# Two transformer blocks on one core: keys of block 2 transposed once a pair and spread by DMA, and 21 weight rests moved to VectorE

## The chip, the core and the metric

The kernel runs on one core of a Trainium2 chip. The time is the device time of one launch in microseconds (us), as the median of several runs. A core has five engines that run their own instruction lists and wait for each other by semaphores: TensorE (PE, matrix products and transposes; PEld is its weight load), VectorE (DVE), ScalarE (ACT), GpSimd (POOL) and SyncE (SP, which here only issues DMA transfers). PE writes to PSUM, from which ACT and DVE bring results to SBUF.

## The reference, cut to what matters

Two transformer blocks of width 1024 work on 512 positions, each with its own weights and with two layers. In the second block, which the change is mostly about, a layer is a pool mixer beside a top-k attention with an index, an output product and an MLP:

```python
def second_block(x, positions, ...):
    for l in range(DEPTH):
        h = rms_norm_2(x, g_pre_mix[l])
        proj = h @ w_in[l]
        u_pool, q, k, v, iq, ik, iw = jnp.split(proj, SPLIT_POINTS, axis=-1)
        q, k, iq, ik = ...                      # rotary positions
        a_out = pool_mixer(u_pool, w_pool[l], pool_scale[l])
        b_out = dsa_attention(q, k, v, iq, ik, iw, topk)
        mix = jnp.concatenate([a_out, b_out], axis=-1) @ w_out[l]
        x = x + rms_norm_2(mix, g_post_mix[l])
        h = rms_norm_2(x, g_pre_ffn[l])
        f = jnp.square(jax.nn.relu(h @ w_ff1[l])) @ w_ff2[l]
        x = x + rms_norm_2(f, g_post_ffn[l])
```

`dsa_attention` has 8 heads of 64. The index scores (`iq`, `ik`, `iw`) choose 128 keys for each query, and each head takes a softmax over these alone. The kernel computes all scores and adds a bias that shuts out the others. The first block has a differential attention beside a recurrent unit, an MLP and a gated product; of it the change touches only the first weights that are converted, at the kernel's start.

## The kernel before

**Numbers in two parts.** PE multiplies in a reduced 32-bit format, so each operand is kept as a rounded part (`hi`, for weights `wh`) and the rest (`lo`, `wl`), and a product is the sum of hi x hi, hi x lo and lo x hi.

**Weights.** `PLAN` lists the pieces of all weights in the order of use, most of them 128x1024. `w_load` (L191) brings a piece by SP into one of three buffers `raw`. `w_conv` (L193) converts it three pieces ahead of its use: ACT makes `wh` (L206), and the rest is made in one of three ways. For pieces of the names in `ON_POOL` and the list `BY_DMA`, ACT writes `-wh` to `wl` (L212) and GpSimd issues a DMA that adds the weight to it from memory (L215). For pieces 1 to 5 GpSimd subtracts in two halves (L219). For all others VectorE subtracts (L131 in the profile, like all of its work). `index` has the weights of the index projection, whose kept pieces are named `F` in layer 1, and `w_out_2` those of the output product; its pieces with `k` from 4 multiply the attention's own heads and come last.

**Block 2's attention.** `mix2` works on four pairs of heads, `j` = 0 to 3. Queries and keys lie as `qk`, four tiles of 128 positions. A score tile is a product of a stacked query `qs` (hi of a head in 64 rows, lo in the other 64) with `ks`, whose two halves hold the key's hi and its lo, each of them twice, in rows 0 to 63 and 64 to 127. `prep_q` transposes the queries of a pair on PE (four transposes, `tpose4`) and stacks them. For keys, `prep_d` lets GpSimd copy a head's 64 columns twice side by side into a tile `xe` (`twice`, L624, four copies a head), and `prep_k` transposes it (`dups`, four transposes a head), ACT copies hi (L634), DVE subtracts lo.

**Order.** PE runs in the order in which the program is written. `weave` mixes the attention's steps with the work of `fill()`, the rest of the projection, the pool mixer and the output product's weights with `k` under 4, so that PE has other matmuls between a tile's scores, its softmax (`sof`: DVE `xe`, ACT `xe`), its transposes (`ptr`: PE, ACT and DVE `pt`) and its product with the values (`pv`). At the end of the loop this other work runs out. The order on the other engines is set by a scheduler with priorities (`urgent` raises one); each engine then works strictly in its order. Pair 0 is prepared ahead of the loop (`run(four(1536, ev_v), ...)`), and pair m + 1 in the steps `r` = 1 to 4 of pair m.

## Time and profile before

| what | us |
|---|---|
| median of 3 runs | 2404.71 (2403.15 to 2405.0) |
| the profiled execution | 2402.2 |
| its span in the trace | 2400.4 |
| PE busy | 2366.5 |
| DVE busy | 1278.5 |
| ACT busy | 1185.3 |
| POOL busy | 220.5 |

The clock that was granted to TensorE is 1.00 over the span. The profile has one execution; its times run from the span's start. The attention loops of block 2 lie at about 1330 to 1420 us (layer 0) and 1915 to 2005 us (layer 1), and the index projection of layer 1 at about 1800 to 1830. A matmul is listed with its start and a modelled duration; starts of neighbours tell PE's pace. In brackets behind a row stands how long the engine was idle just before it and what ended that.

### The profile page before, as it was taken

How to read it: one execution, taken by the hardware profiler on the slowest of the kernel's cores; microseconds unless marked ns; L12 is line 12 of the kernel's file. 1: busy time of each engine (PE TensorE's matmuls, PEld its weight loads, DVE VectorE, ACT ScalarE, POOL GpSimd, SP SyncE). 2: the span in 40 equal slices, each digit the busy share in tenths (PEclk: the TensorE clock that was granted, in tenths of full speed). 3: DMA queues.
4: the chain of work that ended last, by engine and by line, in shares of the span. 5: the costliest groups of instructions: out<-in, count | busy, mean ns of one | idle time of the engine just before them, and what ended most of it. 6: DMA issues, size and time to landing. Idle time of an engine off the chain costs nothing.

```text
span 2400.4 us, 30910 instructions
## 1 busy us (share of the span) xinstructions
PE 2366.5 (99%) x11772; PEld 1975.3 (82%) x11772; DVE 1278.5 (53%) x2548; ACT 1185.3 (49%) x2020; POOL 220.5 (9%) x385
## 2 busy tenths in 40 slices
PE   9999999999999999999999999999999999999999
PEld 6778888888877888888898788888898778888888
DVE  8586433435458643344469857323337975532434
ACT  7785322424678532232366885323337587432422
POOL 3210000000121000000023210000002421000000
PEclk9999999999999999999999999999999999999999
DMA  6744333332874433333257554333336737333231
GB/s 202 173 106 115 97 97 97 96 97 88 193 175 98 114 97 97 97 97 97 84 143 160 119 133 116 97 97 97 97 94 167 176 80 166 97 97 97 88 105 53
DMA packets 80292, 275.69 MB, mean 115 GB/s; under 512 B 8976, under 2 KB 11408, under 8 KB 80144
## 3 DMA queue, kind: packets, MB, share of 16 engines
q1 hardware_dynamic: 62288, 211.22, 27.9%
q0 software_dynamic: 17856, 62.50, 15.0%
q8 instruction: 92, 1.51, 0.3%
q14 instruction: 56, 0.46, 0.1%
HBM read 271.59 MB, written 2.10 MB: 114 GB/s over the span
## 4 chain that ended last, share of the span: by engine, by line
PE 52%; DVE 8%; ACT 5%; DMA 1%; issue 1%; POOL 0%; DVEq 0%; ACTq 0%
PE B L131 52%; DVE ac L131 2%; DVE m L131 2%; ACT xe L686 1%; DMA wl<-in_w 1%; ACT wh L206 1%; ACT xe L1286 1%; DVE X L131 1%; ACT wl L212 1%; ACT pt L1306 1%; DVE fo L131 0%; DVE acc L131 0%; ACT X L1257 0%; DVE h L131 0%; ACT X L398 0%
## 5 line engine op out<-in xcount | busy, mean ns | idle before, releaser
L131 PE MATMUL B<-X,wh 128*128 128x512 f32 (+1 forms) x3200 | 970.8, 386 | 0.0
L206 ACT ACTIVATE wh<-raw 128x1024 fp32r<-128x1024 f32 (+2 forms) x374 | 391.2, 1047 | 802.4 <-PE B L131 774.4
L131 DVE TENSOR_TENSOR wl<-raw,wh 128x1024 fp32r<-128x1024 f32 (+2 forms) x260 | 314.8, 1212 | 714.2 <-ACT wh L206 710.3
L131 PEld LDWEIGHTS B<-X,wh 128*128 128x128 f32 x3200 | 577.8, 188 | 108.6 <-issue 7.3
L131 PE MATMUL B<-X,wl 128*128 128x512 f32 (+1 forms) x1600 | 610.8, 382 | 3.6 <-DMA wl<-in_w 2.0
L131 PE MATMUL B<-F,wh 128*128 128x512 f32 (+1 forms) x2048 | 597.6, 376 | 0.0
L131 PEld LDWEIGHTS B<-F,wh 128*128 128x128 f32 x2048 | 376.4, 188 | 69.8
L131 PE MATMUL B<-F,wl 128*128 128x512 f32 (+1 forms) x1024 | 384.8, 376 | 0.0
L131 PEld LDWEIGHTS B<-X,wl 128*128 128x128 f32 x1600 | 300.8, 188 | 63.8 <-POOL wl L219 2.4
L131 PE MATMUL B<-wh,X 128*128 128x512 f32 (+2 forms) x960 | 288.1, 377 | 0.0
L131 PEld LDWEIGHTS B<-F,wl 128*128 128x128 f32 x1024 | 192.7, 188 | 35.1
L131 PEld LDWEIGHTS B<-wh,X 128*128 128x128 f32 x960 | 174.0, 188 | 31.0 <-issue 1.9
L131 PE MATMUL B<-wl,X 128*128 128x512 f32 (+2 forms) x504 | 178.5, 367 | 0.2 <-ACT X L398 0.2
L215 POOL DMA_DIRECT2D wl<-in_w x105 | 92.1, 877 | 482.0 <-ACT wl L212 329.8
L212 ACT ACTIVATE wl<-raw 128x1024 fp32r<-128x1024 f32 (+2 forms) x111 | 114.5, 1033 | 42.5 <-PE B L131 42.4
L131 DVE TENSOR_TENSOR f<-r 128x512 f32<-128x512 f32 (+1 forms) x136 | 88.4, 657 | 59.6 <-ACT r L589 59.6
L589 ACT ACTIVATE r<-B 128x512 f32<-128x512 f32 (+1 forms) x136 | 76.5, 567 | 80.8 <-PE B L131 78.4
L131 PEld LDWEIGHTS B<-wl,X 128*128 128x128 f32 x504 | 92.1, 188 | 16.5 <-issue 1.9
L131 DVE TENSOR_TENSOR F<-f,F 128x512 fp32r<-128x512 f32 (+1 forms) x136 | 88.5, 656 | 0.9 <-ACT F L395 0.2
L131 PE MATMUL B<-ks,qs 64*128 64x256 f32 (+5 forms) x416 | 80.1, 345 | 5.3 <-DVE on L131 1.8
L395 ACT ACTIVATE F<-f 128x512 fp32r<-128x512 f32 (+1 forms) x136 | 81.3, 603 | 4.4 <-DVE f L131 2.1
L131 DVE TENSOR_TENSOR acc<-acc,q 128x512 f32<-128x512 f32 (+1 forms) x134 | 77.0, 578 | 9.0 <-ACT q L420 5.1
(222 smaller groups left out, 2252.5 us busy)
## 6 DMA issues: line engine op xcount, KB each, us to landing
raw<-in_w SPq DMA_DIRECT2D x379, 512.0 KB, 3.5
wl<-in_w POOLq DMA_DIRECT2D x105, 512.0 KB, 7.8
F<-in_w POOLq DMA_DIRECT2D x8, 512.0 KB, 11.1
raw<-in_wx SPq DMA_DIRECT2D x8, 328.0 KB, 3.3
h<-in_xT SPq DMA_DIRECT2D x8, 256.0 KB, 6.2
raw<-in_wx SPq DMA_DIRECT2D x8, 256.0 KB, 2.7
pt<-in_gates SPq DMA_DIRECT2D x2, 512.0 KB, 5.3
p<-in_pT SPq DMA_DIRECT2D x4, 256.0 KB, 4.9
```

Source lines behind the costliest of these rows:

```text
L131: r = f(*a, **k)
L206: g = A.activation(h_[:, :n], r[:, :n], AF.Copy)
L212: g = A.activation(l_[:, :n], r[:, :n], AF.Copy, scale=-1.0)
L215: G.dma_start(l_[:, :n], where[i], accum_op=OP.add)
L395: A.activation(dst[:, 0, :], src, AF.Copy)
L589: A.activation(r_[:, :n], p_, AF.Relu)
L686: A.activation(e[:, :n], e[:, :n], AF.Exp, scale=-1.0, bias=mn, accum_out=sums)
L1286: A.activation(e[:, :n], e[:, :n], AF.Copy, scale=sm[:, 1:2])
L1306: A.activation(hi, pb, AF.Copy)
```

## The change

It has four parts.

1. The rests of pieces 1 to 5, ten halves of 128x512, are subtracted by VectorE, not GpSimd.
2. Of the index weights of layer 1, three pieces of 128x656 leave `BY_DMA`: VectorE makes their rests, with a raised priority.
3. The pieces of `w_out_2` with `k` from 4, four in each layer, have their rests made by VectorE.
4. For pairs 1 to 3 of block 2, in both layers, `prep_d` and `prep_k` give way to `prep_kk`: the key columns of both heads are transposed together (four transposes), ACT copies hi and DVE subtracts lo once into two tiles `xe`, and eight DMAs on SP (64x512 each) bring each head's rows of hi and lo to both row halves of its `ks`. `prep_q` moves to step 1, `prep_kk` stands in step 2, where `prep_q` stood. Pair 0 stays.

```diff
--- before.py
+++ after.py
@@ -104,7 +104,7 @@
 PLAN = _plan()
 
 BY_DMA = [e for e in PLAN if e[0] == "w_ff1_2" and e[2] in (0, 512)]
-BY_DMA += [e for e in PLAN if e[0] == "index" and e[1] == 0][:3] + [e for e in PLAN if e[0] == "index" and e[1] == 1]
+BY_DMA += [e for e in PLAN if e[0] == "index" and e[1] == 0][:3] + [e for e in PLAN if e[0] == "index" and e[1] == 1 and (e[2] == 0 or e[3] == 0)]
 ON_POOL = ("w_in", "index", "w_in_2", "w_out", "w_out_2")
 
 
@@ -207,6 +207,7 @@
         if "bcast" in st:
             behind(g, st["bcast"].ins)
         if (PLAN[i][0] in ON_POOL and PLAN[i][0] != "index" and i > 5
+                and not (PLAN[i][0] == "w_out_2" and PLAN[i][3] >= 4)
                 and PLAN[i][:4] != ("w_in_2", 0, 512, 0)) or PLAN[i] in BY_DMA:
 
             g = A.activation(l_[:, :n], r[:, :n], AF.Copy, scale=-1.0)
@@ -216,7 +217,7 @@
         elif i <= 5:
             for a in range(0, n, n // 2):
                 b = slice(a, a + n // 2)
-                G.tensor_sub(l_[:, b], r[:, b], h_[:, b].bitcast(F32))
+                V.tensor_sub(l_[:, b], r[:, b], h_[:, b].bitcast(F32))
         else:
             with tc.high_priority(URGENT if PLAN[i][0] == "index" else 0):
                 V.tensor_sub(l_[:, :n], r[:, :n], h_[:, :n].bitcast(F32))
@@ -1097,6 +1098,19 @@
             def prep_k(j, c):
                 st_[j][1][c] = dups(M, kd.pop((j, c)))
 
+            def prep_kk(j):
+
+                p_ = tpose4(qk, 512 + j * 128)
+                hl = [M("xe", F32R) for _ in range(2)]
+                A.activation(hl[0], p_, AF.Copy)
+                V.tensor_sub(hl[1], p_, hl[0].bitcast(F32))
+                for c in range(2):
+                    st_[j][1][c] = M("ks")
+                    for a in range(2):
+                        for b in range(2):
+                            SY.dma_start(st_[j][1][c][64 * b:64 * b + 64, a].bitcast(F32),
+                                         hl[a][64 * c:64 * c + 64].bitcast(F32))
+
             iks = []
 
             def index_k():
@@ -1346,14 +1360,10 @@
                     act(urgent(ptr), j)
                 if 0 <= j - 1 < n and j % 2 == 0:
                     act(urgent(pv), j - 1)
-                if nx and r in (1, 2):
-                    act(prep_d, m + 1, r - 1)
+                if nx and r == 1:
+                    act(urgent(prep_q), m + 1)
                 if nx and r == 2:
-                    act(urgent(prep_q), m + 1)
-                if nx and r == 3:
-                    act(urgent(prep_k), m + 1, 0)
-                if nx and r == 4:
-                    act(urgent(prep_k), m + 1, 1)
+                    act(urgent(prep_kk), m + 1)
             weave(acts, fill(), 66)
         return C[4:8], part
```

Over the whole program PE has 304 transposes of `xe` before and 256 now, and 96 of `qk` before and 120 now. DVE has 12 subtractions `ks` fewer, and 6 of `xe`, 3 of `F`, 8 of `wl` 128x1024 and 10 of `wl` 128x512 more. ACT loses 12 copies `ks`, 3 conversions `F` and 8 `wl` and gains 6 copies `xe`. POOL loses 48 copies `xe<-qk`, 11 DMAs and its 10 subtractions. SP gains 48 DMAs `ks<-xe`.

SP, layer 0, where the keys of pair 1 are made; `raw` are weight loads. Before:

```order
L191 DMA raw_10906<-in_w 128x1024
L191 DMA raw_11014<-in_w 128x1024
L191 DMA raw_11165<-in_w 128x1024
L191 DMA raw_11303<-in_w 128x1024
L191 DMA raw_11460<-in_w 128x1024
L191 DMA raw_11600<-in_w 128x1024
```

Now:

```order
L191 DMA raw_11015<-in_w 128x1024
L191 DMA raw_11163<-in_w 128x1024
L191 DMA raw_11297<-in_w 128x1024
L1111 DMA ks_11029<-xe_11025 64x512 x2
L1111 DMA ks_11029<-xe_11026 64x512 x2
L1111 DMA ks_11034<-xe_11025 64x512 x2
L1111 DMA ks_11034<-xe_11026 64x512 x2
L191 DMA raw_11454<-in_w 128x1024
```

The eight copies of pair 1 stand directly behind a load and ahead of the next one; the first four are the first head's keys.

ACT, layer 0, the end of the attention loop (`xe` softmax, `pt` the transposed probabilities, `X` the pool mixer's output for the product, `wh` and `wl` the last piece of w_out_2). Before:

```order
L1306 ACTIVATE pt_11983<-B_11979 128x3x128
L1286 ACTIVATE xe_11973<-xe_11973,sm_11972 128x512
L1257 ACTIVATE X_11992<-B_11743 128x256
L1257 ACTIVATE X_11990<-B_11744 128x256
L1257 ACTIVATE X_11992<-B_11744 128x256
L1306 ACTIVATE pt_11983<-B_12005 128x4x128
L206 ACTIVATE wh_12041<-raw_11876 128x1024
L212 ACTIVATE wl_12042<-raw_11876 128x1024
L1326 ACTIVATE xe_12020<-B_12000 64x512
```

Now:

```order
L1320 ACTIVATE pt_11959<-B_11955 128x3x128
L1271 ACTIVATE X_11966<-B_11731 128x256
L1271 ACTIVATE X_11968<-B_11731 128x256
L1271 ACTIVATE X_11966<-B_11732 128x256
L1271 ACTIVATE X_11968<-B_11732 128x256
L206 ACTIVATE wh_12017<-raw_11860 128x1024
L1320 ACTIVATE pt_11959<-B_11981 128x4x128
L1340 ACTIVATE xe_11996<-B_11976 64x512
```

The `wl` on ACT is gone, and the last `wh` now stands ahead of the last `pt` (128x4x128) rather than behind it.

DVE at the same place. Before:

```order
L131 TENSOR_TENSOR pt_11932<-B_11964,pt_11932 128x2x128
L131 RECIPROCAL sm_11972<-sm_11972 128x1
L131 TENSOR_TENSOR pt_11983<-B_11979,pt_11983 128x3x128
L131 TENSOR_TENSOR pt_11983<-B_12005,pt_11983 128x4x128
L131 TENSOR_TENSOR ot_11947<-B_12000,xe_12020 64x512
L131 TENSOR_TENSOR X_12023<-ot_11947,X_12023 128x512
```

Now:

```order
L131 RECIPROCAL sm_11927<-sm_11927 128x1
L131 TENSOR_TENSOR pt_11908<-B_11940,pt_11908 128x2x128
L131 RECIPROCAL sm_11948<-sm_11948 128x1
L131 TENSOR_TENSOR pt_11959<-B_11955,pt_11959 128x3x128
L131 TENSOR_TENSOR wl_12018<-raw_11860,wh_12017 128x1024
L131 TENSOR_TENSOR pt_11959<-B_11981,pt_11959 128x4x128
L131 TENSOR_TENSOR ot_11923<-B_11976,xe_11996 64x512
L131 TENSOR_TENSOR X_11999<-ot_11923,X_11999 128x512
```

The last `wl` stands between the two last `pt`.

DVE at the kernel's start (`X` and `acc` are the norm's work on the input `h`, `wl_166` and `wl_173` rests of the second and third piece). Before:

```order
L131 TENSOR_SCALAR cbias<-jp 128x128
L131 TENSOR_TENSOR acc_111<-acc_111,q_149 128x512
L131 RECIPROCAL rcnt<-rcnt 128x16
L131 SCALAR_TENSOR_TENSOR X_130<-h_69,par,X_130 128x512
L131 SCALAR_TENSOR_TENSOR X_133<-h_70,par,X_133 128x512
L131 SCALAR_TENSOR_TENSOR X_136<-h_71,par,X_136 128x512
L131 TENSOR_TENSOR acc_111<-acc_111,q_152 128x512
L131 SCALAR_TENSOR_TENSOR X_139<-h_72,par,X_139 128x512
L131 TENSOR_TENSOR acc_111<-acc_111,q_155 128x512
L131 TENSOR_TENSOR acc_111<-acc_111,q_158 128x512
L131 TENSOR_TENSOR acc_111<-acc_111,q_161 128x512
```

Now:

```order
L131 TENSOR_TENSOR acc_111<-acc_111,q_149 128x512
L131 TENSOR_TENSOR wl_166<-raw_81,wh_165 128x512
L131 SCALAR_TENSOR_TENSOR X_130<-h_69,par,X_130 128x512
L131 SCALAR_TENSOR_TENSOR X_133<-h_70,par,X_133 128x512
L131 SCALAR_TENSOR_TENSOR X_136<-h_71,par,X_136 128x512
L131 TENSOR_TENSOR acc_111<-acc_111,q_152 128x512
L131 SCALAR_TENSOR_TENSOR X_139<-h_72,par,X_139 128x512
L131 TENSOR_TENSOR acc_111<-acc_111,q_155 128x512
L131 TENSOR_TENSOR wl_166<-raw_81,wh_165 128x512
L131 TENSOR_TENSOR acc_111<-acc_111,q_158 128x512
L131 TENSOR_TENSOR wl_173<-raw_170,wh_172 128x512
L131 TENSOR_TENSOR acc_111<-acc_111,q_161 128x512
```

The first half of `wl_166` comes ahead of four `X` and two `acc`, its second half behind them.

## Rows read from the trace of the kernel before

**Rows 1.** The page, part 1: busy us, share, instructions.
```profile
PE 2366.5 (99%) x11772; PEld 1975.3 (82%) x11772; DVE 1278.5 (53%) x2548; ACT 1185.3 (49%) x2020; POOL 220.5 (9%) x385
```

**Rows 2.** Stretches: us, busy by engine, PEclk, DMA share, GB/s.
```profile
1350.00:1375.00 25.00, 23.84 (x133) 19.42 (x132) 22.31 (x60) 21.81 (x48) 5.56 (x16) 1.00 0.41 85
...
1400.00:1420.00 20.00, 17.80 (x103) 14.19 (x102) 9.83 (x30) 19.34 (x45) 2.98 (x6) 1.00 0.46 106
...
1500.00:1795.00 295.00, 295.00 (x1469) 251.40 (x1467) 100.67 (x117) 91.21 (x121) 3.31 (x4) 1.00 0.32 97
```

**Rows 3.** Waits of PE by releaser: total us, times, longest.
```profile
PE B L131 <- DVE pt L131: 4.7, 8, 1.1
...
PE B L131 <- DMA wl<-in_w: 2.0, 2, 1.1
...
PE B L131 <- POOL wl L219: 1.6, 2, 0.8
...
PE B L131 <- POOL sn L406: 0.9, 1, 0.9
...
PE B L131 <- DMA F<-in_wx: 0.6, 2, 0.4
...
PE B L131 <- POOL rs L406: 0.5, 1, 0.5
```

**Rows 4.** Timeline of PE, layer 0: start, duration, instruction, idle before.
```profile
1338.16 0.60 PE L131 MATMUL B<-ident,qk 128*128 128x128 f32 x4
...
1338.52 0.72 PE L131 MATMUL B<-X,wh 128*128 128x512 f32 x2
...
1353.48 0.74 PE L131 MATMUL B<-pt,vv 128*128 128x256 f32 x4 [1.08 <-DVE pt L131]
```

**Rows 5.** Timeline of ACT, layer 0, attention of block 2.
```profile
1338.58 1.04 ACT L212 ACTIVATE wl<-raw 128x1024 fp32r<-128x1024 f32 x1
...
1416.92 0.60 ACT L1306 ACTIVATE pt<-B 128x512 fp32r<-128x512 f32 x1
```

**Rows 6.** Timeline of all engines at the kernel's start.
```profile
0.75 0.39 SPq L363 DMA_DIRECT2D raw<-in_w  x1
...
4.64 0.69 DVE L131 TENSOR_TENSOR wl<-raw,wh 128x512 fp32r<-128x512 f32 x1 [3.20 <-ACT wh L202]
...
8.49 0.75 DVE L131 SCALAR_TENSOR_TENSOR X<-h,par,X 128x512 fp32r<-128x512 f32 x1 [0.67 <-ACT X L398]
...
12.28 3.27 POOL L219 TENSOR_TENSOR wl<-raw,wh 128x512 fp32r<-128x512 f32 x2 [10.22 <-ACT wh L206]
...
13.90 0.50 PE L131 MATMUL B<-X,wl 128*128 128x512 f32 x1 [0.74 <-POOL wl L219]
...
16.75 0.39 PE L131 MATMUL B<-X,wl 128*128 128x512 f32 x1
```

**Rows 7.** DMA issues of the whole span: queue, KB each, us to landing.
```profile
out<-h SPq DMA_DIRECT2D x8, 128.0 KB, 1.8
```

**Rows 8.** Stretches of 2 us behind the transposes of pair 1, layer 0.
```profile
1341.00:1343.00 2.00, 2.00 (x13) 1.69 (x12) 1.96 (x5) 1.63 (x6) 0.00 (x0) 1.00 0.72 244
```

**Rows 9.** Timeline of PE, layer 0, a product of the pool mixer.
```profile
1376.55 1.12 PE L131 MATMUL B<-xe,wp 128*128 128x512 f32 x2 [0.66 <-DVE pt L131]
```

**Rows 10.** The page, part 5: busy us, mean ns, idle before.
```profile
L131 DVE TENSOR_TENSOR wl<-raw,wh 128x1024 fp32r<-128x1024 f32 (+2 forms) x260 | 314.8, 1212 | 714.2 <-ACT wh L206 710.3
```

**Rows 11.** Timeline of PE, layer 0, the end of the attention loop.
```profile
1414.43 0.55 PE L131 MATMUL B<-ident,xe 128*128 128x128 f32 x3 [1.07 <-ACT xe L1286]
...
1417.57 0.38 PE L131 MATMUL B<-pt,vv 128*128 128x256 f32 x1 [0.69 <-ACT pt L1306]
...
1418.30 1.10 PE L131 MATMUL B<-pt,vv 128*128 128x256 f32 x7 [0.34 <-DVE pt L131]
...
1427.90 0.38 PE L131 MATMUL B<-X,wl 128*128 128x256 f32 x1 [1.07 <-DMA wl<-in_w]
```

**Rows 12.** Timeline of DVE at the same place.
```profile
1417.55 0.69 DVE L131 TENSOR_TENSOR pt<-B,pt 128x512 fp32r<-128x512 f32 x1 [1.40 <-ACT pt L1306]
```

## The prediction

> **What bounds the kernel now.** I read the share of busy time first: TensorE is busy in 2366.5 of 2400.4 us, VectorE and ScalarE in about half [rows 1]. Then the stretches: in the MLPs TensorE is busy for 295.00 of 295 us, so nothing that another engine saves there can show. At the end of the attention of block 2 it is busy for 17.80 of 20 us while ScalarE works for 19.34 [rows 2]. So time can come from two places only: from TensorE's own instructions, wherever they stand, and from the few microseconds in which it waits. The waits by releaser say which these are: weight rests brought by GpSimd's accumulating DMA (2.0 us, two times), rests made on GpSimd (1.6, two), VectorE's `pt` (4.7, eight), and small ones at the index projection and the start [rows 3]. The rest of the prediction goes through these waits one by one, since the total of all of them is only a few tens of microseconds.
>
> The profiled run of before took 2402.2 us, 2.5 under the median of the three timed runs, 2404.7. I sum against 2402.2 and add 2.5 at the end.
>
> **The change part by part.**
>
> *Transposes.* A pair of heads now needs one group of four key transposes where it had two. A group stands from 1338.16 to 1338.52, where the next matmul starts [rows 4]: 0.36 us. Three pairs in two layers: 6 x 0.36 = **-2.2 us**, on TensorE itself, so nothing can hide or eat it. The order lists agree: TensorE has 24 transposes fewer in all.
>
> *Copies of the key halves.* In exchange eight transfers of 64x512 a pair go out on SP. Pair 1 is the tight one. The group of key transposes takes the place in which the queries' stood before, so it ends at about 1338.52. ScalarE first makes the rest that stands ahead (1338.58 and 1.04 us [rows 5]), hence 1339.6, then the first half, about 0.6, then VectorE the second, 0.69 [rows 6]: 1340.9. On SP a weight load stands directly ahead, which waits for that same rest; a transfer takes 0.39 us to issue [rows 6], so the fourth of the copies that the first head needs is out at about 1341.7. By the order list TensorE first uses them after six groups of weight matmuls, three score tiles, seven transposes and eight products with the values, 7.05 us at the paces of before, so at about 1345.6. Best case: a 128 KB transfer by itself lands in 1.8 us [rows 7], so 1343.5, and nobody waits. Worst case near at hand: the load (512 KB), the accumulating DMA beside it (512 KB) and the four copies (512 KB) share what the engines moved in 1341 to 1343, 244 GB/s [rows 8]: 1.57 MB take 6.4 us from 1341, so 1347.4, and TensorE waits 1.8. Pair 3 has a load ahead of it as well; pair 2's load is out long before. Between these I take 0.5 for each of the four tight pairs: **+2.0 us**, from 0 to +7.2. Behind the copies, four of which wait for VectorE's half, the next weight load is queued on SP; ScalarE converts its weights several microseconds later, so a wait of 1 us there costs nothing.
>
> The traces show no transfer on 64 rows. [...]
>
> *VectorE and ScalarE in the middle of the attention.* Each pair loses one key copy on ScalarE and one key subtraction of 0.69 on VectorE. Two stalls of each layer end with VectorE's `pt`: 1.08 at 1353.48 [rows 4], and 0.66 at 1376.55 [rows 9], both within the 4.7 us of [rows 3]. VectorE is busy for 22.31 of the 25 us between them [rows 2], so 0.69 less ahead of each should come through: 0.69 + 0.66 a layer, **-2.7 us** in two layers. From 0, should the new subtractions of weights (1.21 each [rows 10]) or a wait of VectorE for a landed copy take the room, to -3.5. The eight copies a pair on GpSimd go too; nobody waited for them, so they count nothing.
>
> *Rests of w_out_2, k from 4.* The last rest of each layer came to TensorE late: 1.07 us at 1427.90, `wl<-in_w` [rows 11], twice [rows 3]. VectorE will have it some 9 us earlier (1418.1, below): **-2.0 us**, sure but for a tenth or two. ScalarE loses four rests a layer, 1.04 each [rows 5]. One of these stood ahead of the softmax whose end TensorE awaits at 1414.43 for 1.07 us [rows 11], so that stall should nearly go. But the order of the change gives it back: the last `wh` now stands ahead of the last `pt` on ScalarE, and the last `wl` ahead of the same `pt` on VectorE. ScalarE's copy, at 1416.92 [rows 5], comes 1.04 earlier for the rest that is gone and as much later for `wh`. VectorE then starts `wl` at about 1416.9, ends it 1.21 later [rows 10] at 1418.1, and its `pt`, at 1417.55 before [rows 12], starts 0.6 later. TensorE's last wait, which ended at 1418.30 [rows 11], ends at 1418.9. The gain of the tail turns into a loss of up to 0.7 a layer; if ScalarE has a gap to make `wh` early, all of 1.07 + 0.69 + 0.34 [rows 11] can go. I take +0.3 a layer: **+0.6 us**, from -4.2 to +1.4. Nothing covers it: TensorE has no weight matmuls between its last transposes and `pt,vv`.
>
> *Index of layer 1.* Three accumulating DMAs and three rests on ScalarE go. TensorE waited 0.6 us for `F<-in_wx` and 0.5 for `rs` there [rows 3], of which the second hangs on the same run of late work. VectorE, now urgent, makes three rests of 128x656, under 1.21 each. They stand among post-norm work that keeps it busy, so one of them may be about a microsecond late: from -1.1 to +1.1, **-0.8 us**.
>
> *Start.* Ten half rests go from GpSimd to VectorE. Two took 3.27 us on GpSimd [rows 6], one takes 0.69 on VectorE. The waits of 1.6 us for `wl` and of 0.9 for `sn`, which came behind these on GpSimd [rows 3], should go but for some tenths: the first half of the first such piece is ready at 13.4, not 13.9, so 0.5 of the 0.74 goes there. The second half is what I fear. VectorE's order has it behind four `X` and two `acc`, 4 x 0.75 + 2 x 0.69 (an `acc` taken like a half rest) = 4.4 us [rows 6], so it is ready at 13.4 + 4.4 + 0.7 = 18.5, and TensorE wants it at 16.75 [rows 6], or 0.5 earlier: a new wait of about 1.9. Sum: 1.9 - 0.5 - 0.85 - 0.9 = **-0.4 us**, from -1.8 to +1.5. Work queued behind the wait on VectorE is `acc`, which nothing on TensorE needs yet.
>
> **The sum:** -2.2 + 2.0 - 2.7 - 2.0 + 0.6 - 0.8 - 0.4 = -5.5 us. The profiled run would take 2396.7 us, the median 2399.2.
>
> **The rivals.**
>
> *A, copies late where a load stands ahead.* Should the four tight pairs wait 1.8 us each, the worst case above, instead of 0.5, 5.2 us come on top: 2404.4. For it: one FIFO on SP, with 1 MB a pair that was not there before, in a stretch whose transfers come in bursts of 244 GB/s [rows 8]. Against it: over the 25 us behind it the engines that move data are busy for 0.41 [rows 2], so a burst is over long before the next pair. Chance 0.15.
>
> *B, copies late at every pair: slower than before.* The place is TensorE's first use of a pair's keys, the price whatever the first head's four copies land behind 1345.6 in pair 1 and its like. At 3 us for each of six pairs it is 18.0 in place of 2.0: 2399.2 + 16.0 = 2415.2. It decides from about 2.1 us at every pair on (12.6 against 2.0, which turns -5.5 into +5.1), so where the copies of pair 1 land after 1347.7, 6 us after the fourth is issued. A 128 KB transfer alone took 1.8 [rows 7]; a load ahead and an accumulate beside it together reach 1347.4 in the tight pairs, so the transfers would have to be dearer than others of their size, and pair 2 as late. Chance 0.10. [...]
>
> *C, VectorE becomes the bound.* It takes over four rests a layer, 4 x 1.21 = 4.8 us, for three subtractions less, 2.1. If the stalls behind `pt` stay (0 for -2.7) and the tail costs its 0.7 a layer (+1.4 for +0.6), it is -2.0: 2402.7. For it: VectorE has little room where the stalls are; the tail's order speaks for it too. Against it: in VectorE's order the four rests of a layer stand behind both stalls. Chance 0.20.
>
> *D, everything comes through.* No copy is late, the tail frees 1.3 a layer, the start gains 1.5, the index 1.1: -2.2 - 2.0 - 2.7 - 2.6 - 1.5 - 1.1 = -12.1, 2392.6. Chance 0.10.
>
> That the change does not do what it says is left out by the order lists: 48 transposes of copied keys go and 24 of `qk` come, 48 copies are on SP, and the eleven accumulating DMAs are gone.
>
> **How the numbers follow.** My forecast has 0.45, at 2399.2, from about 2395 to 2403. This kernel's timing can tell some 0.2%, 4.8 us, from no change: faster is below 2399.9, slower above 2409.5. Faster: more than half of the forecast, 0.30, for some rows have more to give than I took (the index, ScalarE's free time), D (0.10) and some of C and A (0.10), 0.50. Same: the rest of the forecast, of C and of A, 0.40. Slower: B, 0.10. The range from 2392 to 2407 takes in all but B and the ends of the others.
>
> **What would show it.** Right: TensorE's 24 transposes fewer; no wait for `wl<-in_w` near 1427; a wait on `ks` copies of about half a us, under 2 in any case, at the first use of pairs 1 and 3 and none at pair 2; the waits for `pt` at 1353 and 1376 shorter by 0.7; at the start a new wait of about 2 us near 16.5 for `wl` from VectorE, and none at 20.6 and 30.5; near 1418 a wait for VectorE's `pt` that is longer, with `wl` just ahead of it. Wrong: waits at every pair for DMAs `ks<-xe` (B), waits for `raw` on ScalarE because SP's queue is held, or `pt` waits unchanged with VectorE filled by `wl` (C). A forecast that is off by more than 6 us would most likely be off in the copies, the one term with no like in the trace.

## The result: 0.8% slower, and the profile after

The changed kernel took 2422.69 us as the median of four runs (2419.53 to 2424.15), the kernel before beside it 2403.93 (2402.69 to 2405.0): a ratio of 1.0081, 95% interval 1.0069 to 1.0093. It is slower by 18.8 us, where 5.5 less had been forecast. The profiled execution took 2424.15 us, its span is 2422.4, 22.0 longer than before's.

The page's first part answers to [rows 1]:

```profile
PE 2370.7 (98%) x11748; PEld 1982.3 (82%) x11748; DVE 1281.5 (53%) x2563; ACT 1174.1 (48%) x2003; POOL 183.1 (8%) x316
```

TensorE has its 24 transposes fewer. It is idle for 2422.4 - 2370.7 = 51.7 us, where it was 33.9: 17.8 of the 22.0 us are waits. The other 4.2 are busy time, although there is less to do. The waits of TensorE by releaser (total us, times, longest), to set beside [rows 3]:

```profile
PE B L131 <- ACT xe L1300: 17.8, 12, 3.9
PE B L131 <- DMA ks<-xe: 5.6, 3, 3.1
PE B L131 <- DVE pt L131: 3.6, 6, 1.0
PE B L131 <- ACT pt L1320: 3.1, 2, 1.6
PE B L131 <- DVE xe L131: 2.6, 4, 0.8
...
PE B L131 <- ACT X L399: 2.0, 1, 2.0
...
PE B L131 <- DVE wl L131: 1.7, 2, 1.4
```

The waits for GpSimd and for its accumulating DMAs are gone, as intended. In their place come 5.6 us for the copied keys and, as the largest row, 17.8 for ScalarE's `xe`, the softmax. In before that row has 5.5 us in four waits:

```profile
PE B L131 <- ACT xe L1286: 5.5, 4, 2.3
```

**Where the keys are late.** TensorE's timeline in layer 0 (start, duration, instruction, idle before) has the place that the prediction put at 1345.6:

```profile
1347.42 0.40 PE L131 MATMUL B<-X,wl 128*128 128x512 f32 x1
1350.92 1.13 PE L131 MATMUL B<-ks,qs 128*128 128x256 f32 x2 [3.10 <-DMA ks<-xe]
1351.85 1.06 PE L131 MATMUL B<-X,wh 128*128 128x512 f32 x2
1352.71 0.63 PE L131 MATMUL B<-X,wl 128*128 128x512 f32 x1
```

SP's timeline shows the load that is issued just ahead of the copies, and the summary of the eight copies (issues in ns as least, median and most, then us from issue to landing) how late they are:

```profile
1340.79 0.33 SPq L191 DMA_DIRECT2D raw<-in_w  x1
```

```profile
L1111 SPq DMA_DIRECT2D ks<-xe x8: 531/640/1987, 1341.3 to 1348.2; - x8
...
DMA to landing us min/median/max: 4.4/6.9/8.9
```

A copy takes 4.4 to 8.9 us to land and up to 1.99 to issue, so that the eight are issued over some 7 us.

**Where nobody waits for a copy by name.** For pair 2 TensorE has no wait on `ks`, yet the longest wait of the whole trace stands there:

```profile
1376.03 0.40 PE L131 MATMUL B<-ks,qs 128*128 128x256 f32 x2
1380.28 0.55 PE L131 MATMUL B<-ident,xe 128*128 128x128 f32 x3 [3.85 <-ACT xe L1300]
```

VectorE's timeline leads to the cause. The first row is layer 0, the second the same place in layer 1:

```profile
1378.18 0.69 DVE L131 CUSTOM_DVE_ANT_0 xe<-B,ac 128x512 f32<-128x512 f32 x1 [4.28 <-DMA raw<-in_w]
...
1973.84 0.69 DVE L131 CUSTOM_DVE_ANT_0 xe<-B,ac 128x512 f32<-128x512 f32 x1 [3.13 <-DMA ks<-xe]
```

This instruction is a softmax step that writes a new `xe` tile. It reads no `raw`, so the load that the profile names in layer 0 is not what it needs. In layer 1 the releaser is a copy that still reads an old `xe`: the halves hi and lo are kept in tiles of the same name as the softmax's, so a slow copy holds a buffer that VectorE needs, and everything behind it in VectorE's order stands. Of the eight copies the fifth and sixth are the last that read hi. The sixth of pair 2, by itself, in layer 0 and then in layer 1 (issue, then us to landing):

```profile
L1111 SPq DMA_DIRECT2D ks<-xe x1: 1872/1872/1872, 1370.2 to 1370.2; - x1
...
DMA to landing us min/median/max: 7.8/7.8/7.8
...
L1111 SPq DMA_DIRECT2D ks<-xe x1: 2408/2408/2408, 1967.4 to 1967.4; - x1
...
DMA to landing us min/median/max: 6.1/6.1/6.1
```

It lands at 1377.96 and at 1973.51, and VectorE goes on 0.22 and 0.33 us behind it. So it is the tile with hi that was held, in both layers. TensorE then waits 3.85 us in layer 0 and 2.51 in layer 1.

**What a wait costs beyond itself.** Stretches of that time: us, busy by engine, granted clock, DMA share, GB/s.

```profile
1351.00:1353.00 2.00, 1.97 (x5) 1.45 (x6) 0.00 (x0) 0.00 (x0) 0.00 (x0) 0.50 0.09 27
...
1382.00:1384.00 2.00, 2.00 (x8) 1.71 (x8) 1.74 (x4) 2.00 (x6) 0.31 (x1) 0.50 0.00 0
1350.00:1375.00 25.00, 23.00 (x121) 18.97 (x121) 17.85 (x48) 17.22 (x38) 3.19 (x8) 0.93 0.49 103
...
2027.00:2029.50 2.50, 2.50 (x13) 2.50 (x13) 0.38 (x1) 0.59 (x1) 0.00 (x0) 0.50 0.58 210
1949.50:1951.50 2.00, 2.00 (x14) 1.73 (x13) 1.22 (x4) 0.78 (x2) 0.31 (x1) 1.00 0.05 16
```

Behind the idle 3.10 us, and again behind the 3.85, the granted clock is 0.50 for about three microseconds; the matmul pair from 1351.85 takes 0.86 us to the next start where 0.46 to 0.55 is usual. The 25 us in which before had 1.00 [rows 2] have 0.93 here. That is where busy time comes from with less work: 25 x 0.07 = 1.8 us at most for such a stretch, and there are four such falls in the two layers. Not every wait has one, and not every one has a copy ahead of it. It fell behind 3.10, 3.85 and 2.51 us (the last at 1975.94), but not behind 2.25 at 1931.55 or 1.97 at 1948.26, where the last row above has 1.00. The fourth fall, at 2027, stands behind the three waits of layer 1's tail, 1.36, 1.56 and 0.98 us.

### The profile page after: what moved, and what is told of

Its sections match the earlier page's. It is cut to its first block, busy times and chain, and to the rows that moved or that the text cites. A ratio compares the mean times of both kernels' runs of the same rounds, so it can differ in the third digit from the quotient of the medians.

```text
span 2422.4 us, 30927 instructions
## 1 busy us (share of the span) xinstructions
PE 2370.7 (98%) x11748; PEld 1982.3 (82%) x11748; DVE 1281.5 (53%) x2563; ACT 1174.1 (48%) x2003; POOL 183.1 (8%) x316
## 4 chain that ended last, share of the span: by engine, by line
PE 54%; DVE 8%; ACT 4%; DMA 1%; issue 1%; SPq 0%; POOL 0%; DVEq 0%; ACTq 0%
PE B L131 54%; DVE ac L131 2%; DVE m L131 2%; DMA ks<-xe 1%; ACT xe L687 1%; DVE xe L131 1%; ACT xe L1300 0%; DVE X L131 0%; ACT wh L206 0%; DVE fo L131 0%; ACT pt L1320 0%; ACT X L1271 0%; DVE wl L131 0%; DVE acc L131 0%; DVE h L131 0%
## 5 line engine op out<-in xcount | busy, mean ns | idle before, releaser
L131 DVE TENSOR_TENSOR wl<-raw,wh 128x1024 fp32r<-128x1024 f32 (+2 forms) x278 | 330.9, 1192 | 719.1 <-ACT wh L206 715.7
L213 ACT ACTIVATE wl<-raw 128x1024 fp32r<-128x1024 f32 (+2 forms) x103 | 106.1, 1030 | 42.7 <-PE B L131 42.6
L216 POOL DMA_DIRECT2D wl<-in_w x97 | 85.0, 876 | 459.8 <-ACT wl L213 313.1
L131 PEld LDWEIGHTS B<-ks,qs 128*128 128x128 f32 (+1 forms) x416 | 56.0, 188 | 33.4 <-issue 11.3
```

Source lines behind the costliest of these rows:

```text
L131: r = f(*a, **k)
L213: g = A.activation(l_[:, :n], r[:, :n], AF.Copy, scale=-1.0)
L216: G.dma_start(l_[:, :n], where[i], accum_op=OP.add)
```

## The experiments

The theory is that the copied keys lost the time, because they come late beside GpSimd's accumulating DMAs, hold `xe` tiles and slow the clock; the rivals put it on VectorE's new rests, on copies of 64 rows as such, or on the place of the keys' work. The times, against before in the same comparison (medians 2403.84 to 2404.11):

| kernel | us | ratio (95%) |
|---|---|---|
| e1, keys only | 2423.40 | 1.0082 (1.0067 to 1.0097) |
| e2, rests only | 2404.54 | 1.0002 (0.9993 to 1.0012) |
| e3, no accumulate beside the copies | 2409.36 | 1.0025 (1.0015 to 1.0035) |
| e5, plain loads in place of accumulates | 2415.64 | 1.0051 (1.0031 to 1.0071) |
| e13, each plain load twice | 2417.02 | 1.0055 (1.0037 to 1.0074) |
| e4, half of the bytes | 2414.30 | 1.0041 (1.0026 to 1.0056) |
| e7, half of the bytes, no accumulate | 2413.36 | 1.0039 (1.0024 to 1.0054) |
| e8, half by GpSimd, no DMA | 2402.56 | 0.9998 (0.9989 to 1.0008) |
| e9, as e8, a step later | 2402.40 | 0.9993 (0.9984 to 1.0003) |
| e6, start and index only | 2399.74 | 0.9984 (0.9974 to 0.9993) |
| e10, as e6, start urgent | 2400.54 | 0.9986 (0.9977 to 0.9996) |
| e11, as e10, last rests on GpSimd | 2400.58 | 0.9987 (0.9978 to 0.9996) |
| e12, rests only, the last one held back | 2400.19 | 0.9983 (0.9974 to 0.9992) |

**e1 and e2, the change in two halves.** e1 is before with the fourth part alone:

```diff
-                if nx and r == 3:
-                    act(urgent(prep_k), m + 1, 0)
-                if nx and r == 4:
-                    act(urgent(prep_k), m + 1, 1)
+                if nx and r == 2:
+                    act(urgent(prep_kk), m + 1)
```

> The kernel before with the fourth part alone: keys transposed once a pair, halves by eight transfers. Theory (the key copies land 7 to 9 us after the transposes because a load and an accumulating DMA share the transfer engines with them, so TensorE waits for `ks`, and VectorE for the tiles `xe` that the copies still read): all of the loss is here, 2418 to 2428 us, with PE waits for `ks<-xe` of about 5 us and one wait of VectorE for a DMA of about 4 us. First rival (the loss comes from the moved rests, which stand in the way on VectorE and ScalarE): at most 2407 us.

e2 is before with parts 1 to 3 alone, the key work left as it was:

```diff
-                G.tensor_sub(l_[:, b], r[:, b], h_[:, b].bitcast(F32))
+                V.tensor_sub(l_[:, b], r[:, b], h_[:, b].bitcast(F32))
```

> The kernel before with the first three parts alone (rests at the start, of the index and of w_out_2 by VectorE), keys as before. Theory: near the kernel before, 2400 to 2407 us; the end of the attention loops waits some 2 us longer a layer, the waits for `wl<-in_w` (1.1 us a layer) are gone, the start is about 1 us shorter. First rival: 2415 us or more.

The keys alone cost 19.4 us, the rests alone 0.5, which no measurement here tells from nothing: the loss lies in the keys. VectorE's rests as the reason for the loss fall. In e1 TensorE waits 6.5 us for `ks`, in seven places, and 2.10 at pair 2 of layer 0 for the same softmax step as above; there the profile names TensorE's product as the releaser of VectorE, but the sixth copy lands at 1374.82 and VectorE goes on at 1375.03, again 0.22 us behind it.

The 0.5 of e2 is a sum of gains and losses. Parts 1 and 2 alone gain 4.1 us (e6, below), so part 3 loses some 4.8. Besides the tail (under e12) e2 has a wait that before has not, 1.39 us in layer 0 and 1.37 in layer 1:

```profile
1388.29 0.63 PE L131 MATMUL B<-ident,xe 128*128 128x128 f32 x4 [1.39 <-DVE qs L131]
```

On VectorE one of the new rests (`wl`, 1.23 us, at 1385.49) stands just ahead of the queries' `qs`; in before `qs` there makes no one wait. The changed kernel, where `prep_q` comes earlier, does not have this wait.

**e3, no accumulating DMA in the attention.** All rests of w_out_2 go to VectorE:

```diff
-                and not (PLAN[i][0] == "w_out_2" and PLAN[i][3] >= 4)
+                and PLAN[i][0] != "w_out_2"
```

> The changed kernel with all rests of w_out_2 by VectorE, so that no accumulating DMA of w_out_2 runs beside the key copies. Theory: the copies of pairs 1 and 2 land in about 4 us in place of 7 to 10, the waits for `ks<-xe` and VectorE's 4 us wait for a landed copy go, and the time falls by 6 us or more, to 2405 to 2416 us. Second rival (it is not the transfers but the order on ScalarE and VectorE, where the two halves of the keys stand ahead of the softmax): the copies land as late as before or the time stays within 3 us of 2422.7.

13.3 us come back. The copies of the changed kernel and of e3 over the attention of layer 0 (issues, KB each, median us to landing), and the landing of pair 2's eight in e3:

```profile
ks<-xe SPq DMA_DIRECT2D x24, 128.0 KB, 4.8
raw<-in_w SPq DMA_DIRECT2D x5, 512.0 KB, 3.9
wl<-in_w POOLq DMA_DIRECT2D x4, 512.0 KB, 7.9
```

```profile
ks<-xe SPq DMA_DIRECT2D x24, 128.0 KB, 2.4
raw<-in_w SPq DMA_DIRECT2D x6, 512.0 KB, 3.6
...
L1111 SPq DMA_DIRECT2D ks<-xe x8: 467/587/602, 1361.8 to 1366.2; - x8
...
DMA to landing us min/median/max: 2.2/2.3/2.4
```

With GpSimd's accumulates gone the copies land in half of the time, TensorE waits for none, and VectorE for none in front of `xe`. At pair 1 more than this differs: ScalarE no longer makes `-wh` ahead of hi, so the copies go out 0.9 us sooner behind the transposes, and the weight load stands behind them on SP and not ahead. TensorE's place of use in e3:

```profile
1345.52 0.39 PE L131 MATMUL B<-X,wl 128*128 128x512 f32 x1
1345.74 0.40 PE L131 MATMUL B<-ks,qs 128*128 128x256 f32 x2
```

It comes 0.22 us behind the matmul before it, with no wait at all, at 1345.7, and the clock over the 25 us from 1350 is 1.00. So copies on 64 rows are not what is dear; what runs beside them is. Pair 2 of the changed kernel, where no load runs beside the copies, has both cases in one group, from 2.2 to 7.8 us. Its copies and, below, GpSimd's work at that time:

```profile
L1111 SPq DMA_DIRECT2D ks<-xe x8: 461/590/1872, 1367.1 to 1373.4; - x8
...
DMA to landing us min/median/max: 2.2/5.3/7.8
```

```profile
1368.63 0.86 POOL L216 DMA_DIRECT2D wl<-in_w  x1 [3.07 <-ACT X L399]
```

The first three copies, issued before the accumulate was under way, land in about 2.3 us, the five behind them in 5.2 to 7.8, so here copies on SP are late while a transfer of GpSimd's is under way. Pair 3 of layer 0 has a load just ahead and no accumulate, and its eight land in 2.3 to 4.8. e3 is still 5.3 us over before: its waits for the softmax are 12.0 us in place of 5.5, of which more under e8, and the tail's, under e12.

**e5 and e13, are it the bytes or the accumulating?** In e5 the DMAs of w_out_2 on GpSimd load plainly, without adding; the rests then hold whole weights. e13 issues each such load twice.

```diff
-            G.dma_start(l_[:, :n], where[i], accum_op=OP.add)
+            if PLAN[i][0] == "w_out_2":
+                G.dma_start(l_[:, :n], where[i].bitcast(F32R))
+                G.dma_start(l_[:, :n], where[i].bitcast(F32R))
+            else:
+                G.dma_start(l_[:, :n], where[i], accum_op=OP.add)
```

(This is e13; e5 has the second of the two loads left out.)

> The changed kernel, where GpSimd's accumulating DMAs of w_out_2 (k under 4) are plain loads of the same 512 KB into the same tile at the same place, so the rests hold the weights and the values come out wrong; every transfer, wait and byte count from memory stays. It asks whether it is the accumulating that delays the key copies or the further 512 KB. Theory in its first form (the accumulating DMA, which reads its destination and writes it back, holds the transfer engines): the copies land in about 3 us as without it, 2405 to 2413 us. Rival (it is a matter of bytes in the queues): they land in 5 us and more, 2417 us or above.

> As the run with plain loads in place of the accumulating DMAs of w_out_2, but each twice, so 1 MB on GpSimd's queue beside the key copies; the values come out wrong in the same way. An accumulating DMA moves its 512 KB in and also reads what it adds to. If the delay of the key copies goes by the bytes that the transfer engines handle, two loads act like one accumulating DMA: copies of pair 1 land 6 to 8 us after their issue, 2419 to 2425 us. If it is the accumulating itself, they stay near the run with one load, under 6 us, 2413 to 2418.

The same stretch in e5 and then e13:

```profile
ks<-xe SPq DMA_DIRECT2D x24, 128.0 KB, 4.6
wl<-in_w POOLq DMA_DIRECT2D x4, 512.0 KB, 5.0
```

```profile
wl<-in_w POOLq DMA_DIRECT2D x8, 512.0 KB, 4.8
...
ks<-xe SPq DMA_DIRECT2D x24, 128.0 KB, 5.8
```

e5 differs from the changed kernel in the accumulating alone, and is 7.0 us faster; an accumulate takes 7.9 us to land where a load of the same size takes 5.0. The other 6.3 of the 13.3 us lie between e5 and e3, and are the load's only in part, since e3 also takes the `-wh` from ScalarE and lets the copies out sooner. e5 has the held tile too: VectorE waits 2.05 us for copies `ks<-xe` in layer 0 and goes on 0.22 us behind the sixth copy.

By the median of all 24, two loads make the copies land later than the accumulates do. But the four for which TensorE waits first, those of the first head of pair 1, land in 7.8 to 8.9 us in the changed kernel, 5.8 to 6.0 in e5 and 6.2 to 6.8 in e13. So twice the bytes move them by less than a microsecond, and accumulating by 2 to 3. The traces of the two attention loops, from TensorE's first wait for `xe` to its first in front of `X,F`, agree: over before they take 20.6 us more in the changed kernel, 15.8 in e5, 16.5 in e13 and 9.9 in e3. What of an accumulate does the rest stays open. Each of e5 and e13 has only two runs, those of e13 6.7 us apart (2413.66 and 2420.39), so these two can't be told from each other by their times.

**e4 and e7, half of the bytes by DMA.** ScalarE and VectorE make each head's halves in the rows where the head lies, and one DMA a head brings both to the other rows. e4 has this in place of the eight copies; e7 has parts 1 and 2 beside it and all w_out_2 rests on VectorE, so no accumulate is near. Its main lines are:

```diff
+                    A.activation(k_[o, 0], p_[o], AF.Copy)
+                    V.tensor_sub(k_[o, 1], p_[o], k_[o, 0].bitcast(F32))
+                    SY.dma_start(k_[x].bitcast(F32), k_[o].bitcast(F32))
```

> The kernel before with the fourth part in another form: ScalarE and VectorE write each head's hi and lo directly into its own 64 rows of `ks` (two operations of 64x512 for each engine, in place of one of 128x512), and one transfer of 64x1024 a head brings them to the other 64 rows. So half the bytes, two transfers a pair, and no tile `xe` is held by a transfer. Theory: VectorE no longer waits for landed copies, TensorE's waits for `ks` shrink below 3 us in all: 2400 to 2411 us. Second rival: the order is as before or worse (one more operation on each engine), so 2418 us or more.

> Parts 1 and 2, keys in the form of half copies (own half by ScalarE and VectorE, one 64x1024 transfer a head), and all rests of w_out_2 by VectorE, so that nothing but weight loads shares the queues with the copies. Theory: the copies land in about 3 us, no waits for `ks` are left, and what stays is the order on ScalarE and VectorE: 2402 to 2408 us. If it is below 2400, the order was not at fault either.

e4 gains 9.1 us on e1. No tile `xe` is held any more, but the six transfers of 256 KB in layer 0 land in 3.3 to 7.5 us, and TensorE waits 5.9 for two, one in each layer. In e7 they land in 4.3 at the median and TensorE waits 0.7 for one, and yet it is hardly faster. Four instructions of 64x512 stand there on ScalarE and VectorE where e3 has two of 128x512, ahead of the softmax. e7 is 4 us behind e3 and outside of what was expected. The traces don't put that down to the keys: the two attention loops take 10.3 us more than before in e7 and 9.9 in e3. What differs is the index projection, where e7 waits 1.53 us for `X` and e3 0.50, with the clock at 0.50 behind it in e7 alone (over the span it is 0.997 in e7 and 0.999 in e3); whether that holds for the other runs is not shown.

**e8 and e9, no DMA at all.** GpSimd copies the half to the other rows; e9 puts queries and keys one step later.

```diff
-                    SY.dma_start(k_[x].bitcast(F32), k_[o].bitcast(F32))
+                    G.tensor_copy(k_[x], k_[o].bitcast(F32))
```

> Parts 1 and 2, keys transposed once a pair, own half by ScalarE and VectorE, and the other 64 rows copied by GpSimd (one operation of 64x1024 a head) in place of any DMA; w_out_2 as before, with its accumulating DMAs. Theory (transfers beside accumulating DMAs are the fault): no key is late, the saved transposes come through, 2398 to 2403 us. Second rival (the order of the two key halves on ScalarE and VectorE costs as much): 2405 us or more. A third way: GpSimd's copies stretch VectorE's work beside them.

> As the run with the other half by GpSimd, but `prep_q` in step 2 and the keys in step 3, where they stood before the change (`prep_k` of the first head). It asks whether the order on VectorE and ScalarE is what remains. If the earlier place of the key halves, ahead of softmax steps that are ready, costs the rest (the new waits for `xe` from ScalarE of 1.7 us in pair 1 to 2): 2397 to 2401 us. If the remaining loss is at the loop's end alone (1.5 and 1.7 us a layer), which the place does not touch: 2402 to 2404.

Both are level with before. They have parts 1 and 2 beside the keys, and e6, which has these two alone, is at 2399.74. So even without a transfer the shared keys, as built here, bring nothing, and by the medians cost 2.8 us (the intervals overlap a little), though TensorE has 2.2 us less to do. e8's waits show where it goes:

```profile
PE B L131 <- ACT xe L1296: 11.0, 10, 2.2
...
PE B L131 <- DVE pt L131: 2.6, 8, 0.4
```

The waits for `pt` have shrunk from 4.7 to 2.6, as the prediction wanted, but those for the softmax have doubled, from 5.5 in e6 to 11.0. Two reasons for the loss can be read. One is that the halves of the key stand ahead of ready softmax steps. VectorE in the changed kernel, at pair 1:

```profile
1341.36 0.69 DVE L131 TENSOR_TENSOR xe<-B,xe 128x512 fp32r<-128x512 f32 x1 [0.95 <-ACT xe L1105]
1341.96 0.28 DVE L131 CUSTOM_DVE_ANT_0 xe<-B,kbias 128x128 f32<-128x128 f32 x1
```

It idles 0.95 us for ScalarE's hi, subtracts, and only then does the softmax step for which TensorE waits 1.15 at 1343.76. That place is one of several, and moving the keys by a step (e9) left the time as it was. The other is the end of the loop. In e8, e9 and e1, too, ScalarE's last `wh` stands ahead of the last `pt`, though part 3 is not in them, and TensorE's three waits there are 1.36, 1.56 and 0.34 us where e6 has 1.09, 0.69 and 0.34: 2.3 us more waiting in the two layers, not far from the 2.8. e12, below, shows that this order can be mended; e8 with that mended was not run, so what the shared keys would be worth then is open.

**e6 and e10, start and index.** e6 is before with parts 1 and 2. e10 raises the priority of the start's rests:

```diff
-                G.tensor_sub(l_[:, b], r[:, b], h_[:, b].bitcast(F32))
+                with tc.high_priority(URGENT):
+                    V.tensor_sub(l_[:, b], r[:, b], h_[:, b].bitcast(F32))
```

> The kernel before with parts 1 and 2 alone (rests at the start and of the index by VectorE). From the stalls of the run with the first three parts: start -1.1 us, index -1.7, so 2400 to 2402.5 us against 2404.0; the tail's part is then +2.2 for both layers. If the parts act on each other, 2403 to 2405.

> Parts 1 and 2, with the start's rests raised in priority, so that both halves of the second piece stand ahead of the four `X` and two `acc` on VectorE. If my reading of the start is right (a new wait of 1.4 us because the second half stands behind these), the wait goes and nothing else moves: 1 to 1.5 us less than parts 1 and 2 without it, 2398 to 2400.5 us, or some of it is given back where `X` comes 0.7 us later.

e6 is 4.1 us faster than before, the best of all. e10 removes the wait of 1.44 us for `wl` at the start and gets another in its place:

```profile
23.21 1.05 PE L131 MATMUL B<-ones,acc 128*128 128x1 f32 x8 [1.27 <-DVE acc L131]
```

So the order on VectorE there only chose which of its work was late.

**e11 and e12, the tail.** e11 is e10 with the last rests of w_out_2 subtracted on GpSimd; e12 is e2 with the last `wh` held behind the last `pt` on ScalarE. Both edits are shown in part; e12 also puts off the conversion of that piece until the pieces with `k` under 4 are used.

```diff
+        elif PLAN[i][0] == "w_out_2" and PLAN[i][3] >= 4:
+            G.tensor_sub(l_[:, :n], r[:, :n], h_[:, :n].bitcast(F32))
```

> As the run with the start's rests raised, and the rests of w_out_2 with k from 4 subtracted by GpSimd in one operation (in place of VectorE, as in the change, or of ScalarE and an accumulating DMA, as before). If the loss of the third part is that VectorE's rests stand ahead of the last `pt`, and the gain is the rest that is no longer 8 us in an accumulating DMA, this keeps the gain alone: 2 to 4 us less than without, 2395 to 2398 us. If the tail is bound by ScalarE's `wh` ahead of `pt`, or GpSimd's work stretches VectorE's, it stays or rises.

```diff
+        if PLAN[i][0] == "w_out_2" and PLAN[i][2:4] == (512, 6):
+            behind(g, st["pt"].ins)
```

> Parts 1, 2 and 3 (keys as before), with one thing changed: in each layer the last piece's `wh` on ScalarE, and with it VectorE's `wl`, stands behind the last `pt` of the attention and not ahead of it. In the run of the three parts TensorE waits 1.35, 1.56 and 0.99 us at the loop's end. If the order that I read there is the cause, the second and third waits shrink to under 0.7 and 0.4, and with the wait for `wl<-in_w` gone too the time is 2396 to 2399.5 us, below parts 1 and 2 alone. If the waits stay, it is the chain from TensorE over ScalarE and VectorE itself, and the time is 2402 to 2405.

e11 is level with e10, where 2 to 4 us less had been expected: whether GpSimd adds by DMA or subtracts itself makes no difference that can be measured. Its 1.5 us of waits for `wl<-in_w` are gone, but the waits for ScalarE's `pt` have gone from 1.4 to 3.1. For e12, first TensorE at the end of layer 0's attention in e2, then the same in e12:

```profile
1414.61 0.55 PE L131 MATMUL B<-ident,xe 128*128 128x128 f32 x3 [1.35 <-ACT xe L1287]
...
1418.33 0.38 PE L131 MATMUL B<-pt,vv 128*128 128x256 f32 x1 [1.56 <-ACT pt L1307]
1419.70 1.10 PE L131 MATMUL B<-pt,vv 128*128 128x256 f32 x7 [0.99 <-DVE pt L131]
```

```profile
1414.17 0.55 PE L131 MATMUL B<-ident,xe 128*128 128x128 f32 x3 [1.35 <-ACT xe L1292]
...
1417.02 0.38 PE L131 MATMUL B<-pt,vv 128*128 128x256 f32 x1 [0.69 <-ACT pt L1312]
1417.74 1.10 PE L131 MATMUL B<-pt,vv 128*128 128x256 f32 x7 [0.34 <-DVE pt L131]
```

The two last waits are back at 0.69 and 0.34, their size of before [rows 11]. The spans differ by 2.5 us, the medians by 4.3. Still e12 is not below e6, as had been expected: the waits behind `qs`, 1.39 and 1.38 us, are in it as in e2.

## Why the prediction was wrong

**The step that failed is the price of the copies**, +2.0 us with +7.2 as its upper end. With it, the transposes and `pt` the keys were to gain 2.9 us; kernel e1 puts their whole net at +19.4. The use came where it was expected (1345.7 in e3), but TensorE could go on only at 1350.9, 3.5 us after the worst case near at hand. Three things were wrong in it.

- The bound shared the bytes of load, accumulate and copies at 244 GB/s [rows 8], as if a transfer cost its bytes. Such transfers among themselves take 2.2 to 2.4 us (pair 2 of e3), close to the 1.8 taken [rows 7]; beside an accumulate the same copy takes up to 8.9. The accumulate itself takes 7.9 us to land and a load of its size from the same queue 5.0. The issues, taken at 0.39 each [rows 6], took up to 1.99 in pair 1, and the fourth copy was out at 1343.6 and not at 1341.7.
- The text counted who waits for the copies, and not who waits for what the copies read. Both halves lie in `xe` tiles, which the softmax of the same loop reuses, and VectorE stood 4.28 and 3.13 us for them. This put the longest wait into pair 2, which the prediction held to be safe: 3.85 + 2.51 = 6.4 us on TensorE, more than its 5.6 for the copies by name. That the tiles were `xe` stood in the change.
- A wait was priced at its own length. Behind those of 3.10, 3.85 and 2.51 us the clock was at 0.50 for some three more.

Rival B, slower than before, had the sign (2415.2 at a chance of 0.10). Its condition, copies of pair 1 landing after 1347.7, held. Its mechanism did not hold in full: TensorE waited for `ks` three times, all at pair 1 of a layer, and not at six pairs. Its objection to itself, that the copies would have to be dearer than other transfers of their size, asked the right question: alone they hardly are, beside an accumulate they are. While e3's copies alone run they move 203 GB/s, with the DMA engines at 0.91. Whether 64 rows have a part in that rate is not shown: SP issued these copies about 0.63 us apart, and 128 KB in 0.63 us is some 210 GB/s by itself. In e3 this rate made nobody wait.

```profile
1363.00:1365.00 2.00, 1.23 (x7) 0.77 (x5) 2.00 (x9) 1.50 (x6) 0.00 (x0) 1.00 0.91 203
```

**The other steps.**

- Transposes: 24 fewer, as counted. But "nothing can hide or eat it" was wrong: e8 has them fewer too and is no faster, since TensorE then waits for the softmax and at the loop's end.
- `pt` in the middle, -2.7: the wait at 1353 is gone in the changed kernel, and `pt` as a whole went from 4.7 to 3.6 us (2.6 in e8). The gain did not come through: waits for `xe` grew, which the prediction did not list as the next thing to be late.
- `wl<-in_w` at the end: gone in both layers, 2.0 us, as forecast.
- The tail: the mechanism was right, its size not. Forecast were +0.3 a layer and at most +0.7; e2's rows give (1.35 - 1.07) + (1.56 - 0.69) + (0.99 - 0.34) = +1.8. The first wait did not go with the rest that ScalarE lost: in e2 the next tile's exponential (`xe<-xe,mn`, 0.73 us) stands ahead of the step that TensorE awaits. And `wh` pushed `pt` by 0.9 us rather than taking the place of the rest; for the second and third wait e12 shows this order to be the cause. Left out of the sum was the wait behind `qs`, 1.4 us a layer in e2: rival C's mechanism, VectorE's rests in the way, at a place that C did not name. In the changed kernel it does not show.
- Start, -0.4: as read. The second half came late, 1.44 us where 1.9 was expected, in the changed kernel:

```profile
18.08 0.50 PE L131 MATMUL B<-X,wl 128*128 128x512 f32 x1 [1.44 <-DVE wl L131]
```

- Index, -0.8: the waits for `F<-in_wx` and `rs` (1.1 us) are gone, and one of 0.5 for `X` stands there in e3 and e6, so about right. In the changed kernel this one is 2.0 at 1818, since ScalarE stood for a load, and the clock is at 0.50 behind it for some three microseconds; in e11 it is 1.1, in e12 1.2, in e7 and e13 1.5. Why the load is late in some of the kernels was not tried.

```profile
1817.26 0.75 ACT L206 ACTIVATE F<-raw 128x656 fp32r<-128x656 f32 x1 [2.10 <-DMA raw<-in_wx]
```

Start and index together were put at -1.2; e6 gives -4.1, with an interval from -6.2 to -1.7 us. Its profiled execution took 2402.3, the slowest of its runs. In it the granted clock is 0.50 for some three microseconds at 1239 and at 1919 and 0.998 over the span, where before has 1.00, so its rows can't show the whole of that gain. These two parts are what there is of gain in the change. Kernel e6 with them alone, and e12 with the tail's order mended, beat both kernels: by 0.16 and 0.17% the one before, by 0.95% and 0.93% the changed one.

## What to carry to other kernels

Price a copy that replaces compute with what shares the DMA engines in its few microseconds, an accumulating DMA above all, and not by its bytes alone: here a copy of 128 KB landed in 2.2 to 2.4 us among its like and in up to 8.9 beside a load and an accumulate. A tile that a transfer read stayed taken until it had landed (VectorE's write went on 0.22 and 0.33 us behind that), so ask which engine next writes to that pool and what stands behind that write in its order; keep such tiles out of a pool that the critical loop turns over. And where TensorE ran at 99%, taking transposes from it shortened nothing, so name the next wait in line before such a gain is counted.

## What the runs showed of the hardware

- A 64x512 copy from SBUF to SBUF lands in 2.2 to 2.4 us when only others like it run (pair 2 of e3), in 2.3 to 4.8 behind a load of 512 KB (pair 3 of layer 0 of the changed kernel), and in 4.4 to 8.9 beside a load and an accumulate of 512 KB each (pair 1). An accumulate of 512 KB takes 7.9 us to land (median) where a plain load, issued by the same queue, takes 5.0 (e5).
- SP's issue of such a copy takes 0.47 to 0.60 us in pair 2 of e3, where no other transfer runs, and up to 1.99 in layer 0 and 2.41 in layer 1 of the changed kernel, so the issuing engine falls behind as well.
- Behind idles of 3.10, 3.85, 2.51 and 2.01 us in the changed kernel TensorE's granted clock was 0.50 for about three microseconds, and 1.00 again after that. Behind idles of 2.25 and 1.97 us it stayed at 1.00.
- VectorE's write to a tile that copies still read went on 0.22 us (layer 0) and 0.33 us (layer 1) behind the landing of the last copy that read it, at pair 2 of the changed kernel, and 0.22 us behind it at the same place of layer 0 in e1 and e5.
